# Scan branch of a decoder trunk: a new order for its gates, its state caches and its elementwise steps

## The chip, the cores and the metric

The kernel runs on one core of one Trainium2 chip. The metric is the device time of one execution in microseconds (us). A core has TensorE (PE) for matrix products, VectorE (DVE), ScalarE (ACT) and GpSimd (POOL) for elementwise work, and SyncE (SP), which here issues all bulk DMAs. Each engine works through its own queue in order; semaphores tie the queues together.

## The reference

Two layers, each an FFN half-step, a mixer and a second FFN half-step, on 288 columns: 256 prompt tokens and 8 samples of 4 tokens. The mixer has three branches; the change is in the second.

```python
h = rmsnorm(x);  u_pool, z, xbc, dt, q_mem, g = split(h @ w_in)
y_pool = pool_mix(u_pool)                      # branch 0: trailing windows 2/4/8/16
xs, B, C = silu(causal_conv(xbc))              # branch 1: Mamba-2 scan, 16 heads x 64, state 128
y, h_last = ssd_scan(xs, dt, a, B, C, h0)      # prompt: decays exp(seg); samples: h0 scaled, plus B x
y_ssm = grouped_rmsnorm((y + d_skip * xs) * silu(z)) * ssm_norm
y_mem = mem_attend(q_mem, k, v)                # branch 2: cross-attention
merged = sum_b sigmoid(g_b + bias_b) * (y_b @ w_br_b)
x = x + merged @ w_o
```

## The kernel before

**Weights.** All weights come in slabs of eight 128x128 tiles, 512 KB each, on SP's queue (`raw`). ACT copies a slab rounded into `whi` (L137) and DVE subtracts it from `raw` into `wlo` (L145). A tile is three products of 128x288 (`mm3`, L246): `whi` by the high part of the input, `whi` by its low part, `wlo` by the high part. So a slab is 24 products on PE.

**Order.** Nothing schedules at run time. `Stream.tick` runs ahead of every slab: it issues the load five slabs ahead, the split of the next slab, then `step()`, which takes one step of every work item on a list, in the list's order, then further splits. All small work (the scan, the attention, gates) is generators on this list; an item started with a delay `d` waits `d` slabs. What an item issues on PE stands ahead of the slab's own 24 products, as one burst.

**The mixer's slabs,** counted from the first `u` slab as r0: `u` r0 to r3, `z` r4 to r11, then per branch the gate columns g and the branch products b: g0/b0 r12 to r23, g2/b2 r24 to r35, g1/b1 r36 to r51, `o` r52 to r59. In each, b(c) follows two gates behind g(c).

**The scan's items.** `heads4(g)`, four of them, started with delays 4, 8, 12, 16: turn xs (`ps_x`), put the sums of the log decays in PSUM (`rows`, `ps_row`), scale by dt (`xd`, DVE) and by the decay to the end (`xw`, POOL), then per pair of heads clamp on DVE (`E<-ps_row,nact`, 128x512) and exponentials on ACT (`decay`), multiply by the masked C·B product (`E<-E,cbm`, DVE), products `ps_y`, finish (`xs<-xs,vec,ps_y`, `st`). `sample_state(b)`, eight of them, delays 8+2b: load a 512 KB state `hb`, mask B for the sample (`bm`, POOL), product `ps_yo` of the old state, scale the state by `Ee` (POOL, 128x1024), add the product `ps_up` (`hb<-hb,ps_up`, DVE), store. `sample_diag` (delay 7), `sample_y` (27) and `group_norm` (30; eight steps that end in the split inputs `ysh`, `ysl` of b1) follow.

**Shared buffers.** `xd`, `xw`, `bm`, the pooling branch's `pw` (POOL, L991 on), the attention's `pr` and `pp` come from one pool of five buffers of 128x512 ("t2"). PSUM has seven banks for all of this.

Of the kernel before, what the change touches and what calls it, by code (L numbers as in the profile page):

```python
# [15 lines left out]
KC = D // P  # L16
# [53 lines left out]
def mixer_groups():  # L70
    def w(kind, c, base, n=KC):
        return kind, (c,), [("w_in", base + c * P)], (n,)

    yield "q", (0, 1, 2, 3), [("w_in", C_Q + c * P) for c in range(4)], FIRST
    for c in list(range(8, 16)) + list(range(8)):
        yield w("xbc", c, C_XBC)
    for c in range(4):
        yield w("u", c, C_POOL)
    for c in range(8):
        yield w("z", c, C_Z)  # L80
    for br, name, n in ((0, "w_br_pool", 4), (2, "w_br_mem", 4), (1, "w_br_ssm", KC)):
        for c in range(KC + 2):
            if c < KC:
                yield w(f"g{br}", c, C_G + br * D)
            if c >= 2:
                yield f"b{br}", (c - 2,), [(name, (c - 2) * P)], (n,)
    yield "o", (0, 1, 2, 3), [("w_o", c * P) for c in range(4)], FIRST
    for c in range(4, 8):
        yield "o", (c,), [("w_o", c * P)], (KC,)
# [96 lines left out]
def trunk_kernel(ctx, tc, wpack, xT, memT, vecs, consts, wdt, wpool, hpool, hconv, h0T, kT, vC,  # L186
# [61 lines left out]
    def act(out, a, func, **kw):  # L248
        A.activation(out=out, in_=a, func=func, **kw)  # L249
# [344 lines left out]
    def mixer(i, cur, nxt):  # L594
# [65 lines left out]
        def dt_work(ps_dt):  # L660
# [71 lines left out]
            mm(pe[:, :TP], par, sb[32:32 + H, :])  # L732
            mm(pd[:, :P], ones[64:64 + H, :], sb[64:64 + H, :P])
            mm(pr[1][:, :TP], ones[96:96 + H, :], sb[96:96 + H, :])
            V.tensor_copy(out=nact[:, 0:2].rearrange("p a h -> p (a h)"), in_=pt[:, :2 * H])
            V.tensor_copy(out=nact[:TS, 2], in_=pt[:TS, 2 * H:3 * H])
            yield
            V.tensor_copy(out=Eb.rearrange("p a t -> p (a t)"), in_=pe[:, :256])
# [84 lines left out]
        def sample_state(b):  # L823
            hb = k4.tile([P, D], F32, tag="k4", name="hb")
            nc.sync.dma_start(out=hb, in_=h0T[i, b])
            yield
            bm = wide("bm", 96, 512, F32R)
            tt(bm, Bst.bitcast(F32), con[:96, K_BM + b:K_BM + b + 1].to_broadcast([96, 512]), ALU.mult, G)
            yield
            if b == 0:  # L830
                yo.append(sum_bank("ps_yo"))
            for g in range(4):
                mm(yo[0][TS * g:TS * g + TS, :256], block(cm, g, b), hb[:, g * 256:(g + 1) * 256], b == 0, b == DB - 1)
            h3 = hb.rearrange("p (h d) -> p h d", h=H)
            tt(h3, h3, Ee[:, b, :].unsqueeze(2).to_broadcast([P, H, 64]), ALU.mult, G)
            pu = [bank("ps_up0"), bank("ps_up1")]
            for g in range(4):
                mm(pu[g // 2][:, (g % 2) * 256:(g % 2 + 1) * 256], bm[:, g * P:(g + 1) * P],
                   xst[g // 2][:, (g % 2) * 256:(g % 2 + 1) * 256])
            yield  # L840
            if b == DB - 1:
                ysb = wide("ysb", P, 256)
                act(ysb, yo[0][:, :256], AF.Copy)
            for q in range(2):
                tt(hb[:, q * 512:(q + 1) * 512], hb[:, q * 512:(q + 1) * 512], pu[q], ALU.add)
            yield
            nc.sync.dma_start(out=o_ssm_s[i, b], in_=hb)
            if b == DB - 1:
                pt = bank("ps_yot")
                for j in range(2):  # L850
                    PE.transpose(pt[:, j * P:(j + 1) * P], ysb[:, j * P:(j + 1) * P], ident)
                yield
                Y4, E4 = (v.rearrange("p (g j) t -> p j g t", j=2) for v in (yoff, Eb))
                tt(Y4, pt[:, :256].rearrange("p (j g t) -> p j g t", j=2, g=4), E4, ALU.mult)

        def heads4(g):

            hs = slice(4 * g, 4 * g + 4)

            def rows(pi):  # L860
                prow = bank("ps_row")
                for j in range(2):
                    h = 4 * g + 2 * pi + j
                    mm(prow[:, j * TP:(j + 1) * TP], sel2[:, h:h + 1].to_broadcast([P, P]), nst)
                return prow

            def clamp(pi, prow):
                E = ep.tile([P, 2, 3 * P], F32, tag="E", name="E")
                h = 4 * g + 2 * pi
                nh = nact[:, 0:2, h:h + 2].rearrange("p t j -> p j t").unsqueeze(3).to_broadcast([P, 2, 2, P])  # L870
                tt(E.rearrange("p j (a t) -> p j a t", a=3)[:, :, 0:3:2, :],
                   prow.rearrange("p (j a t) -> p j a t", j=2, a=2), nh, ALU.max)
                return E

            def decay(pi, prow, E):
                for j in range(2):
                    h = 4 * g + 2 * pi + j
                    act(E[:, j, P:TP], prow[:, j * TP + P:(j + 1) * TP], AF.Exp, scale=-1.0, bias=b01[:, h:h + 1])
                    for t_ in range(2):
                        e = E[:, j, TP * t_:TP * t_ + P]  # L880
                        act(e, e, AF.Exp, scale=-1.0, bias=nact[:, t_, h:h + 1])

            def outputs(Es):

                ys = [bank("ps_y") for _ in Es]
                for pi, E in enumerate(Es):
                    for k in range(2):
                        for j in range(2):
                            x0 = k * TP + 128 * pi + 64 * j
                            mm(ys[pi][64 * j:64 * j + 64, k * P:TP], xd[:, x0:x0 + 64],  # L890
                               E[:, j, k * TP:k * TP + (2 - k) * P], k == 0, k == 1)
                for pi in range(2):
                    for k in range(2):
                        x0 = k * TP + 128 * pi
                        mm(ys[pi][:, 320:448], xw[:, x0:x0 + P], Bt[:, k, g * P:(g + 1) * P], k == 0, k == 1)
                return ys

            def finish(pi, py):
                p = 2 * g + pi
                xp = chunk(xsu, p)[:, :TP]  # L900
                st = tmp("st", P)
                stt(xp, xp, col(i, V_DS, p), py[:, :TP], ALU.mult, ALU.add)
                act(st, py[:, 320:448], AF.Copy)
                nc.sync.dma_start(out=o_ssm_p[i, p], in_=st)

            px = bank("ps_x")
            for t_ in range(2):
                for pi in range(2):
                    k = t_ * TP + pi * P
                    PE.transpose(px[:, k:k + P], chunk(xsu, 2 * g + pi)[:, t_ * P:(t_ + 1) * P], ident)  # L910
            r0 = rows(0)
            yield
            xd, xw = wide("xd"), wide("xw")
            xd4 = xd.rearrange("p (t h d) -> p t h d", t=2, h=4)
            tt(xd4, px.rearrange("p (t h d) -> p t h d", t=2, h=4),
               dtt[:, 0:2, hs].unsqueeze(3).to_broadcast([P, 2, 4, 64]), ALU.mult)
            tt(xw.rearrange("p (t h d) -> p t h d", t=2, h=4), xd4,
               wt[:, 0:2, hs].unsqueeze(3).to_broadcast([P, 2, 4, 64]), ALU.mult, G)
            E0 = clamp(0, r0)
            r1 = rows(1)  # L920
            yield
            E1 = clamp(1, r1)
            decay(0, r0, E0)
            decay(1, r1, E1)
            yield
            for E in (E0, E1):
                tt(E, E, cbm[:, g, :].unsqueeze(1).to_broadcast([P, 2, 3 * P]), ALU.mult)
            yield
            ys = outputs((E0, E1))
            yield  # L930
            finish(0, ys[0])
            finish(1, ys[1])
# [252 lines left out]
        for kind, cs, tiles, cuts in mixer_groups():  # L1185
# [9 lines left out]
                ym.extend(unit(f"ym{j}") for j in range(2))  # L1195
            if kind == "u" and c == 0:
                items["xss"] = W.start(xss_work(), 3)
                items["ss"] = [W.start(sample_state(b), 8 + 2 * b) for b in range(DB)]
                items["pairs"] = [W.start(heads4(g), 4 + 4 * g) for g in range(4)]
                items["pairs"].append(W.start(sample_diag(), 7))  # L1200
                items["yo"] = W.start(sample_y(), 27)
                items["gn"] = W.start(group_norm(), 30)
            if kind == "z" and c == 0:
                W.finish(items["conv"])
            if kind == "g2" and c == 0:
# [43 lines left out]
                items["dt"] = W.start(dt_work(ps_dt))  # L1249
            elif kind[0] == "g":  # L1250
                br = int(kind[1])
                gates[br, c] = tmp("gate")
                W.start(gate(br, c, ps[0], gates[br, c]))
            elif kind[0] == "b":
                W.start(merge(int(kind[1]), c, ps[0]))
            else:
                if norm is None:
                    norm = Norm(*nxt)
                W.start(x_update(cs, ps, norm))
# [125 lines left out]
```

## Time and profile before

| | us |
| --- | --- |
| median of three runs (lowest, highest) | 1559.61 (1558.95, 1559.99) |
| the profiled execution | 1559.71 |
| its span in the trace | 1557.6 |
| PE busy | 1533.0 (98%) |
| DVE busy | 1068.2 (69%) |
| ACT busy | 801.9 (51%) |
| POOL busy | 240.3 (15%) |

The span is the time from the first to the last instruction in the trace; the execution's own time is 2.1 us longer. Busy shares are averages over the FFN and mixer stages. Where an engine stood idle, the profile names what ended the idle time ("<-").

### The profile page before, as it was taken

What the parts mean: (1) busy time and instruction counts of PE and PEld (TensorE: products, weight loads), DVE (VectorE), ACT (ScalarE), POOL (GpSimd) and SP (SyncE); (2) the same over time, 40 slices, a digit from 0 to 9 for tenths busy, and PEclk for the clock granted to TensorE, in tenths of its full rate; (3) what the DMA queues carried; (4) which work ended last, traced back from release to release, by engine and by line L of the source; (5) the groups of instructions that cost most, each with busy time, mean ns of one, the idle gap of its engine ahead of it and who ended that gap; (6) DMA issues with size and microseconds to landing.
All of it is one profiled execution on the core that took longest, in us unless ns stands there. A gap on an engine that the chain in (4) does not pass through costs nothing.

```text
span 1557.6 us, 29192 instructions
## 1 busy us (share of the span) xinstructions
PE 1533.0 (98%) x11736; PEld 1492.8 (96%) x11736; DVE 1068.2 (69%) x1666; ACT 801.9 (51%) x1232; POOL 240.3 (15%) x324
## 2 busy tenths in 40 slices
PE   9999999999999999999999999999999999999997
PEld 7999999898889999999999999999988999999997
DVE  7766655898878767665566665579887776766643
ACT  7544444575655545444445444457556555544442
POOL 0100001245233111000000000024522310200001
PEclk9999999999999999999999999999999999999998
DMA  8644445565565545454545444546565655444551
GB/s 298 216 169 163 162 163 169 204 226 188 201 222 169 168 152 177 163 164 167 170 150 176 163 164 166 182 172 228 186 236 177 202 162 163 163 164 166 167 167 72
DMA packets 80711, 278.00 MB, mean 178 GB/s; under 512 B 9024, under 2 KB 13248, under 8 KB 80576
## 3 DMA queue, kind: packets, MB, share of 16 engines
q1 hardware_dynamic: 79872, 275.28, 52.4%
q8 instruction: 92, 1.51, 0.4%
q10 hardware_dynamic: 704, 0.86, 0.2%
q14 instruction: 43, 0.35, 0.1%
HBM read 262.39 MB, written 13.71 MB: 177 GB/s over the span
## 4 chain that ended last, share of the span: by engine, by line
PE 90%; DVE 5%; ACT 2%; POOL 1%; DMA 1%; issue 1%; DVEq 0%; ACTq 0%; POOLq 0%
PE ps L246 65%; PE pd L246 18%; PE ps_v L246 1%; POOL pw L234 1%; DVE wlo L145 1%; PE ps_y L246 1%; PE ps_k L246 1%; ACT whi L137 1%; DVE cacc L243 1%; PE ps_up L246 1%; PE ps_yo L246 1%; ACT L249 0%; DMA raw<-wpack 0%; PE ps_cb L246 0%; DVE E L234 0%
## 5 line engine op out<-in xcount | busy, mean ns | idle before, releaser
L145 DVE TENSOR_TENSOR wlo<-raw,whi 128x1024 fp32r<-128x1024 f32 (+1 forms) x441 | 551.6, 1252 | 257.7 <-ACT hidh L249 100.0
L137 ACT ACTIVATE whi<-raw 128x1024 fp32r<-128x1024 f32 (+1 forms) x441 | 464.0, 1054 | 313.9 <-PE ps L246 137.8
L246 PE MATMUL ps<-n1h,whi 128*128 128x288 f32 x896 | 270.4, 302 | 5.3 <-DVE cbuf L234 3.5
L246 PE MATMUL ps<-n1l,whi 128*128 128x288 f32 x896 | 264.9, 296 | 0.0
L246 PE MATMUL ps<-n1h,wlo 128*128 128x288 f32 x896 | 264.3, 295 | 0.6 <-DVE wlo L145 0.6
L246 PE MATMUL ps<-n2h,whi 128*128 128x288 f32 x704 | 208.8, 297 | 0.0
L246 PE MATMUL ps<-n0h,whi 128*128 128x288 f32 x704 | 208.8, 297 | 0.0
L246 PE MATMUL pd<-hidh,whi 128*128 128x288 f32 x704 | 208.4, 296 | 0.0
L246 PE MATMUL ps<-n2l,whi 128*128 128x288 f32 x704 | 207.7, 295 | 0.0
L246 PE MATMUL pd<-hidl,whi 128*128 128x288 f32 x704 | 207.7, 295 | 0.0
L246 PE MATMUL ps<-n0l,whi 128*128 128x288 f32 x704 | 207.7, 295 | 0.0
L246 PE MATMUL ps<-n0h,wlo 128*128 128x288 f32 x704 | 207.0, 294 | 0.0
L246 PE MATMUL ps<-n2h,wlo 128*128 128x288 f32 x704 | 207.0, 294 | 0.0
L246 PE MATMUL pd<-hidh,wlo 128*128 128x288 f32 x704 | 207.0, 294 | 0.0
L246 PEld LDWEIGHTS ps<-n1h,whi 128*128 128x128 f32 x896 | 168.7, 188 | 8.1 <-issue 5.1
L246 PEld LDWEIGHTS ps<-n1h,wlo 128*128 128x128 f32 x896 | 169.2, 189 | 0.8 <-DVE wlo L145 0.8
L246 PEld LDWEIGHTS ps<-n1l,whi 128*128 128x128 f32 x896 | 168.9, 189 | 0.5
L234 POOL TENSOR_TENSOR acc<-acc,sqr 128x288 f32<-128x288 f32 x42 | 45.9, 1092 | 797.4 <-ACT sqr L249 796.3
L246 PEld LDWEIGHTS pd<-hidh,wlo 128*128 128x128 f32 x704 | 132.6, 188 | 0.0
L246 PEld LDWEIGHTS ps<-n0h,wlo 128*128 128x128 f32 x704 | 132.6, 188 | 0.0
L246 PEld LDWEIGHTS ps<-n2h,wlo 128*128 128x128 f32 x704 | 132.6, 188 | 0.0
L246 PEld LDWEIGHTS ps<-n2l,whi 128*128 128x128 f32 x704 | 132.2, 188 | 0.1
(309 smaller groups left out, 2749.1 us busy)
## 6 DMA issues: line engine op xcount, KB each, us to landing
raw<-wpack SPq DMA_DIRECT2D x439, 512.0 KB, 3.3
cb<-kT SPq DMA_DIRECT2D x16, 512.0 KB, 5.6
cb<-vC SPq DMA_DIRECT2D x16, 512.0 KB, 4.7
hb<-h0T SPq DMA_DIRECT2D x16, 512.0 KB, 6.0
o_ssm_s<-hb SPq DMA_DIRECT2D x16, 512.0 KB, 5.0
x<-xT SPq DMA_DIRECT2D x4, 288.0 KB, 5.6
o_mk<-ksb SPq DMA_DIRECT2D x2, 512.0 KB, 5.7
o_mv<-vsb SPq DMA_DIRECT2D x2, 512.0 KB, 4.9
```

Source lines behind the costliest of these rows:

```text
L137: nc.scalar.activation(out=hi[:, a], in_=self.loaded[self.n_hi][:, a], func=AF.Copy)
L145: nc.vector.tensor_tensor(out=lo[:, a], in0=raw[:, a], in1=self.his[n][:, a].bitcast(F32), op=ALU.subtract)
L234: (eng or V).tensor_tensor(out=out, in0=a, in1=b, op=op)
L243: V.scalar_tensor_tensor(out=out, in0=a, scalar=s, in1=b, op0=op0, op1=op1)
L246: PE.matmul(out, lhsT=lhsT, rhs=rhs, start=start, stop=stop)
```

## The change

1. In the g1/b1 stage all eight gates go first (r36 to r43), then the eight products b1 (r44 to r51). Before, b1(0) stood at r39. The eight gates are kept in four buffers of the pool of units instead of the small temporaries.
2. Delays: `sample_diag` 7 to 6 and to the list's head, `heads4` 4+4g to 7+4g, `sample_state` 8+2b to 14+2b and behind the heads in the list, `sample_y` 27 to 33, `group_norm` 30 to 36.
3. From POOL to DVE: the scaling of the state (`hb<-hb,Ee`, 8 a layer) and `xw` (4 a layer). From POOL to ACT: `bm` (8 a layer).
4. From DVE to ACT: the clamp (8 a layer). `max(row, nact)` becomes four `Relu(row - nact)` of 128x128 straight from PSUM (`nact` is stored negated), and the four exponentials of these blocks become one of 128x512. The exponentials of the middle blocks stay. Both run in the step that made the rows' successor.

```diff
-    for br, name, n in ((0, "w_br_pool", 4), (2, "w_br_mem", 4), (1, "w_br_ssm", KC)):
-        for c in range(KC + 2):
+    for br, name, n, lag in ((0, "w_br_pool", 4, 2), (2, "w_br_mem", 4, 2), (1, "w_br_ssm", KC, KC)):
+        for c in range(KC + lag):
...
-            V.tensor_copy(out=nact[:, 0:2].rearrange("p a h -> p (a h)"), in_=pt[:, :2 * H])
+            ts(nact[:, 0:2].rearrange("p a h -> p (a h)"), pt[:, :2 * H], -1.0, ALU.mult)
...
-            tt(bm, Bst.bitcast(F32), con[:96, K_BM + b:K_BM + b + 1].to_broadcast([96, 512]), ALU.mult, G)
+            act(bm, Bst.bitcast(F32), AF.Copy, scale=con[:96, K_BM + b:K_BM + b + 1])
...
-            tt(h3, h3, Ee[:, b, :].unsqueeze(2).to_broadcast([P, H, 64]), ALU.mult, G)
+            tt(h3, h3, Ee[:, b, :].unsqueeze(2).to_broadcast([P, H, 64]), ALU.mult)
...
-                tt(E.rearrange("p j (a t) -> p j a t", a=3)[:, :, 0:3:2, :],
-                   prow.rearrange("p (j a t) -> p j a t", j=2, a=2), nh, ALU.max)
...
+                    for t_ in range(2):
+                        act(E[:, j, TP * t_:TP * t_ + P], prow[:, j * TP + P * t_:j * TP + P * t_ + P], AF.Relu,
+                            bias=nact[:, t_, h:h + 1])
                     act(E[:, j, P:TP], prow[:, j * TP + P:(j + 1) * TP], AF.Exp, scale=-1.0, bias=b01[:, h:h + 1])
-                    for t_ in range(2):
-                        e = E[:, j, TP * t_:TP * t_ + P]
-                        act(e, e, AF.Exp, scale=-1.0, bias=nact[:, t_, h:h + 1])
+                e = E.rearrange("p j (a t) -> p j a t", a=3)[:, :, 0:3:2, :]
+                act(e, e, AF.Exp, scale=-1.0)
...
-               wt[:, 0:2, hs].unsqueeze(3).to_broadcast([P, 2, 4, 64]), ALU.mult, G)
+               wt[:, 0:2, hs].unsqueeze(3).to_broadcast([P, 2, 4, 64]), ALU.mult)
...
-                items["ss"] = [W.start(sample_state(b), 8 + 2 * b) for b in range(DB)]
-                items["pairs"] = [W.start(heads4(g), 4 + 4 * g) for g in range(4)]
-                items["pairs"].append(W.start(sample_diag(), 7))
-                items["yo"] = W.start(sample_y(), 27)
-                items["gn"] = W.start(group_norm(), 30)
+                items["pairs"] = [W.start(sample_diag(), 6)] + [W.start(heads4(g), 7 + 4 * g) for g in range(4)]
+                items["ss"] = [W.start(sample_state(b), 14 + 2 * b) for b in range(DB)]
+                items["yo"] = W.start(sample_y(), 33)
+                items["gn"] = W.start(group_norm(), 36)
...
-                gates[br, c] = tmp("gate")
+                if br == 1 and c % 2 == 0:
+                    held = unit("gates")
+                gates[br, c] = held[:, c % 2, :] if br == 1 else tmp("gate")
```

**Place one: DVE's queue in slabs r4 to r6 of a layer,** where the pooling branch's windows (`pw` from POOL, `pd` on DVE) meet the scan's first heads. Before:

```order
L145 TENSOR_TENSOR wlo<-raw,whi 128x1024
L234 TENSOR_TENSOR xd<-ps_x,dtt 128x512
L234 TENSOR_TENSOR E<-ps_row,nact 128x2x2x128
L243 SCALAR_TENSOR_TENSOR pd<-pw,ub_4218 128x256
L243 SCALAR_TENSOR_TENSOR pd<-pw,ub_4218 128x32
L234 TENSOR_TENSOR pf<-pw,con 128x3
L234 TENSOR_TENSOR pd<-pf,ub_4218 128x3
L234 TENSOR_TENSOR z_4400<-ps,R_n_2450 128x288
L145 TENSOR_TENSOR wlo<-raw,whi 128x1024
L234 TENSOR_TENSOR xst_4339<-xss_4338,xst_4339 32x512
L234 TENSOR_TENSOR xst_4343<-xss_4342,xst_4343 32x512
L234 TENSOR_TENSOR E<-ps_row,nact 128x2x2x128
```

And now:

```order
L145 TENSOR_TENSOR wlo<-raw,whi 128x1024
L243 SCALAR_TENSOR_TENSOR pd<-pw,ub_4218 128x256
L243 SCALAR_TENSOR_TENSOR pd<-pw,ub_4218 128x32
L234 TENSOR_TENSOR pf<-pw,con 128x3
L234 TENSOR_TENSOR pd<-pf,ub_4218 128x3
L234 TENSOR_TENSOR z_4392<-ps,R_n_2450 128x288
L145 TENSOR_TENSOR wlo<-raw,whi 128x1024
L234 TENSOR_TENSOR xst_4339<-xss_4338,xst_4339 32x512
L234 TENSOR_TENSOR xst_4343<-xss_4342,xst_4343 32x512
L243 SCALAR_TENSOR_TENSOR pd<-pw,ub_4266 128x256
```

`xd` has left this place (it now stands at r8, behind all four `pd`), and the clamps `E<-ps_row,nact` are gone from DVE.

**Place two: DVE's queue from a scaling of attention weights (`pr`) in the g0/b0 stage,** with the state's adds (`hb<-hb,ps_up`) and the next heads. Before:

```order
L1037 RECIPROCAL sm<-sm 128x2
L238 TENSOR_SCALAR pr<-pr,sm 128x256 x2
L1030 TENSOR_REDUCE mx<-ps_sp 128x2
L238 TENSOR_SCALAR mx<-mx 128x2
L234 TENSOR_TENSOR hb<-hb,ps_up_4862 128x512
L234 TENSOR_TENSOR hb<-hb,ps_up_4863 128x512
L243 SCALAR_TENSOR_TENSOR xs_3001<-xs_3001,vec,ps_y 128x256 x2
L234 TENSOR_TENSOR xd<-ps_x,dtt 128x512
L234 TENSOR_TENSOR E<-ps_row,nact 128x2x2x128
L234 TENSOR_TENSOR gate<-ps,R_n_2450 128x288
L145 TENSOR_TENSOR wlo<-raw,whi 128x1024
```

And now:

```order
L1032 RECIPROCAL sm<-sm 128x2
L238 TENSOR_SCALAR pr<-pr,sm 128x256 x2
L1025 TENSOR_REDUCE mx<-ps_sp 128x2
L238 TENSOR_SCALAR mx<-mx 128x2
L234 TENSOR_TENSOR gate<-ps,R_n_2450 128x288
L145 TENSOR_TENSOR wlo<-raw,whi 128x1024
L243 SCALAR_TENSOR_TENSOR xs_3001<-xs_3001,vec,ps_y 128x256 x2
L234 TENSOR_TENSOR xd<-ps_x,dtt 128x512
L234 TENSOR_TENSOR xw<-xd,wt 128x512
L234 TENSOR_TENSOR hb<-hb,Ee 128x1024
L234 TENSOR_TENSOR part_4956<-ps,gate 128x288
L145 TENSOR_TENSOR wlo<-raw,whi 128x1024
```

The next heads' steps and the state's adds have moved from the slab of `pr` to its neighbours, and `xw` and the scaling `hb<-hb,Ee` stand on DVE.

**Place three: ACT's queue at a group's decays.** Before, the first group's (at r6):

```order
L249 ACT_TABLE_LOAD
L249 ACTIVATE E<-ps_row,b_3008 128x128
L249 ACTIVATE E<-E,nact 128x128 x2
L249 ACTIVATE E<-ps_row,b_3008 128x128
L249 ACTIVATE E<-E,nact 128x128 x2
L249 ACTIVATE E<-ps_row,b_3008 128x128
L249 ACTIVATE E<-E,nact 128x128 x2
L249 ACTIVATE E<-ps_row,b_3008 128x128
L249 ACTIVATE E<-E,nact 128x128 x2
L137 ACTIVATE whi<-raw 128x1024
```

And now, from the first group's first pair (at r8):

```order
L249 ACTIVATE E<-ps_row,nact 128x128 x2
L249 ACT_TABLE_LOAD
L249 ACTIVATE E<-ps_row,b_3008 128x128
L249 ACTIVATE E<-ps_row,nact 128x128 x2
L249 ACTIVATE E<-ps_row,b_3008 128x128
L249 ACTIVATE E<-E 128x2x2x128
L249 ACTIVATE yph_4135<-ps_pool,vec 128x288
L137 ACTIVATE whi<-raw 128x1024
L249 ACTIVATE E<-ps_row,nact 128x128 x2
```

A pair of heads now has seven activations instead of six, one of them four blocks wide, and its two pairs stand in two slabs instead of one. The program's loads of activation tables go from 48 to 52.

## Rows read from the trace of the kernel before

**Rows 1.** PE's waits by line waited for: us in total, times, longest us.

```profile
PE ps L246 <- DVE cbuf L234: 3.5, 2, 1.8
PE ps_y L246 <- DVE E L234: 3.1, 2, 1.9
PE ps_row L246 <- DVE hb L234: 2.2, 2, 1.1
PE ps L246 <- DVE hb L234: 1.8, 2, 0.9
PE ps_row L246 <- DVE xs L234: 1.5, 1, 1.5
...
PE ps L246 <- DVE wlo L145: 0.6, 1, 0.6
```

**Rows 2.** PE's timeline, first layer, slab r7: start, us, instruction, [idle before <-releaser].

```profile
376.53 0.51 PE L246 MATMUL ps<-n1h,whi 128*128 128x288 f32 x1
376.87 0.29 PE L246 MATMUL ps<-n1l,whi 128*128 128x288 f32 x1
377.75 0.40 PE L246 MATMUL ps<-n1h,wlo 128*128 128x288 f32 x1 [0.58 <-DVE wlo L145]
377.98 0.30 PE L246 MATMUL ps<-n1h,whi 128*128 128x288 f32 x1
...
380.65 0.29 PE L246 MATMUL ps<-n1h,wlo 128*128 128x288 f32 x1
382.87 2.02 PE L246 MATMUL ps_y<-E,xd 128*64 128x256 f32 x16 [1.93 <-DVE E L234]
```

**Rows 3.** Windows: length; busy us (instructions) by engine; granted clock, DMA share, GB/s.

```profile
384.37:387.78 3.41, 3.41 (x19) 2.77 (x15) 3.20 (x12) 0.96 (x2) 0.00 (x0) 0.50 0.60 196
410.70:458.37 47.67, 46.55 (x358) 41.73 (x359) 38.23 (x59) 35.24 (x71) 14.17 (x10) 1.00 0.55 191
1053.75:1057.16 3.41, 3.41 (x15) 3.41 (x16) 3.34 (x9) 2.21 (x5) 1.93 (x5) 0.55 0.90 347
```

**Rows 4.** DVE's and POOL's timelines, first layer, slabs r3 to r7.

```profile
359.84 1.74 POOL L234 TENSOR_TENSOR pw<-ub 128x422 f32<-128x422 f32 x1
...
366.28 0.89 POOL L234 TENSOR_TENSOR pw<-ub 128x422 f32<-128x422 f32 x1
...
372.67 0.69 DVE L234 TENSOR_TENSOR xd<-ps_x,dtt 128x512 f32<-128x512 f32 x1 [6.62 <-POOL pw L234]
...
379.04 0.69 DVE L234 TENSOR_TENSOR E<-ps_row,nact 128x512 f32<-128x512 f32 x1
```

**Rows 5.** DVE's and POOL's timelines at the same moment of the g0/b0 stage.

```profile
406.25 2.90 DVE L238 TENSOR_SCALAR pr<-pr,sm 128x256 f32<-128x256 f32 x2
406.05 1.90 POOL L234 TENSOR_TENSOR hb<-hb,Ee 128x1024 f32<-128x1024 f32 x1 [5.59 <-PE ps_yo L246]
```

**Rows 6.** Groups by line and shape, first layer's r0 on: count | busy, mean ns | idle before.

```profile
L145 DVE TENSOR_TENSOR wlo<-raw,whi 128x1024 fp32r<-128x1024 f32 x47 | 59.8, 1273 | 3.0 <-PE ps L246 2.4 <-ACT whi L137 0.6
L234 POOL TENSOR_TENSOR hb<-hb,Ee 128x1024 f32<-128x1024 f32 x8 | 16.4, 2055 | 48.5 <-PE ps_yo L246 48.5
L249 ACT ACT_TABLE_LOAD x10 | 12.8, 1283 | 4.7 <-PE ps_pv L246 3.2 <-DVE rs L240 1.1 <-issue 0.3
L249 ACT ACTIVATE E<-E,nact 128x128 f32<-128x128 f32 x32 | 11.0, 398 | 0.0
L238 DVE TENSOR_SCALAR pr<-pr,sm 128x256 f32<-128x256 f32 x8 | 10.1, 1296 | 0.1
L234 POOL TENSOR_TENSOR bm<-Bst,con 96x512 fp32r<-96x512 f32 x8 | 8.5, 1063 | 0.3 <-ACT E L249 0.3
L243 DVE SCALAR_TENSOR_TENSOR ysl<-z,vec,ysh 128x288 fp32r<-128x288 f32 x8 | 4.7, 646 | 0.0
L234 POOL TENSOR_TENSOR xw<-xd,wt 128x512 f32<-128x512 f32 x4 | 4.4, 1089 | 21.8 <-DVE xd L234 21.8
L249 ACT ACTIVATE z<-z 128x576 f32<-128x576 f32 x4 | 2.4, 674 | 0.0
```

More of the change, by code (lines that the diff above doesn't have):

```diff
@@ L80, in mixer_groups @@
         yield w("z", c, C_Z)
-    for br, name, n in ((0, "w_br_pool", 4), (2, "w_br_mem", 4), (1, "w_br_ssm", KC)):
-        for c in range(KC + 2):
+    for br, name, n, lag in ((0, "w_br_pool", 4, 2), (2, "w_br_mem", 4, 2), (1, "w_br_ssm", KC, KC)):
+        for c in range(KC + lag):
             if c < KC:
                 yield w(f"g{br}", c, C_G + br * D)
-            if c >= 2:
-                yield f"b{br}", (c - 2,), [(name, (c - 2) * P)], (n,)
+            if c >= lag:
+                yield f"b{br}", (c - lag,), [(name, (c - lag) * P)], (n,)
     yield "o", (0, 1, 2, 3), [("w_o", c * P) for c in range(4)], FIRST
@@ L865, in rows, with decay @@
                 return prow
-            def clamp(pi, prow):
+            def decay(pi, prow):
                 E = ep.tile([P, 2, 3 * P], F32, tag="E", name="E")
-                h = 4 * g + 2 * pi
-                nh = nact[:, 0:2, h:h + 2].rearrange("p t j -> p j t").unsqueeze(3).to_broadcast([P, 2, 2, P])
-                tt(E.rearrange("p j (a t) -> p j a t", a=3)[:, :, 0:3:2, :],
-                   prow.rearrange("p (j a t) -> p j a t", j=2, a=2), nh, ALU.max)
-                return E
-            def decay(pi, prow, E):
                 for j in range(2):
                     h = 4 * g + 2 * pi + j
+                    for t_ in range(2):
+                        act(E[:, j, TP * t_:TP * t_ + P], prow[:, j * TP + P * t_:j * TP + P * t_ + P], AF.Relu,
+                            bias=nact[:, t_, h:h + 1])
                     act(E[:, j, P:TP], prow[:, j * TP + P:(j + 1) * TP], AF.Exp, scale=-1.0, bias=b01[:, h:h + 1])
-                    for t_ in range(2):
-                        e = E[:, j, TP * t_:TP * t_ + P]
-                        act(e, e, AF.Exp, scale=-1.0, bias=nact[:, t_, h:h + 1])
+                e = E.rearrange("p j (a t) -> p j a t", a=3)[:, :, 0:3:2, :]
+                act(e, e, AF.Exp, scale=-1.0)
+                return E
             def outputs(Es):
@@ L917, in heads4 @@
             tt(xw.rearrange("p (t h d) -> p t h d", t=2, h=4), xd4,
-               wt[:, 0:2, hs].unsqueeze(3).to_broadcast([P, 2, 4, 64]), ALU.mult, G)
-            E0 = clamp(0, r0)
+               wt[:, 0:2, hs].unsqueeze(3).to_broadcast([P, 2, 4, 64]), ALU.mult)
+            E0 = decay(0, r0)
             r1 = rows(1)
             yield
-            E1 = clamp(1, r1)
-            decay(0, r0, E0)
-            decay(1, r1, E1)
+            E1 = decay(1, r1)
             yield
```

## Prediction

> **What bounds the kernel now.** I began with the table of busy times: PE is busy 1533.0 us of a span of 1557.6, so the elementwise engines matter only where PE waits for them. Second came PE's waits by line [rows 1]. The reader should see that not all of them are in reach. The 3.5 us for `cbuf` belong to the convolution, which the change leaves alone. The other five rows shown (E, hb twice, xs, wlo; eight waits in two layers) lie in the stretch that is rewritten: 3.1 + 2.2 + 1.8 + 1.5 + 0.6 = 9.2 us.
>
> Third, PE's timeline around the worst of them, to see what a wait costs from start to start [rows 2]. Products follow each other every 0.133 us (from 377.98 to 380.65 twenty steps), so a slab of 24 is 3.2 us. From 380.65 to 382.87 it is 2.22 us, that is 2.09 lost, where the row names 1.93: idle time is counted from a modelled end, 0.16 behind the pitch. Eight waits therefore cost 9.2 + 8 x 0.16 = **10.5 us**.
>
> Fourth, the granted clock in windows [rows 3]. Just behind the 2-us wait of layer 0, TensorE ran 3.41 us at 0.50, the lower of its two levels (1.2 GHz); before it PE had idled. The same work at full clock takes half, so this costs **1.7 us**. A second stretch, 3.41 us at 0.55, follows the untouched convolution wait of layer 1.
>
> Fifth, why DVE is late. Two causes show. In r5 and r6 DVE stands 6.62 us until POOL finishes `pw` [rows 4]: `xd` needs a buffer of the pool that the windows `pw` fill, and everything behind it, the clamps, the next `wlo`, E, is late by as much. Later, in the attention's slabs, the two scalings `pr` of 128x256 take 2.90 us, and the first of them begins 0.2 us after POOL's state scaling, which runs 1.90 us [rows 5]. An operation of 128x512 takes 0.69 on DVE [rows 4], so a 128x256 should need about 0.4 (an estimate from that row and the 1.27 of 128x1024); the eight average 1.296 [rows 6]. These slabs also carry the state's adds and the next heads in the old order, and the `hb` waits of PE stand right behind.
>
> **The change, part by part.**
>
> *Later heads.* `xd` goes to r8, behind all four `pd`, where POOL's windows are over. DVE then waits for POOL only in `pd`, one `pw` chain at a time, and `wlo` is not behind the last chain. That removes the E and `wlo` waits of layer 0 and the E and xs waits of layer 1: 3.1 + 1.5 + 0.6, with four times 0.16 5.8 us, and the clock's 1.7 with the wait ahead of it. Next late in these slabs is POOL's own chain: the same operations in the same slabs, and the products that need it (`ps_pool`) are in their old places. For that I keep 0.5 us a layer, **+1.0** in all; the ends are 0 (no wait shows at `ps_pool` in rows 1) and half of the 5.8.
>
> *POOL's work to DVE and ACT.* Per layer DVE gets 8 scalings of 128x1024 at 1.27 (the row of `wlo`, same size [rows 6]) and 4 `xw` at 0.69 [rows 4]: 10.2 + 2.8. It loses 8 clamps at 0.69, 5.5, and if `pr` falls from 1.296 to 0.4 in eight cases, 7.2. The sum is near zero, +0.3 us a layer, against 16.4 + 8.5 + 4.4 that POOL no longer needs [rows 6]. What counts is the spread: by the order, the adds, heads and scalings now stand in different slabs than `pr`. So the four `hb` waits (2.2 + 1.8 + four times 0.16 = 4.6 us) go. Bounds: if `pr` stays at 1.296 for a reason of its own, DVE has +7.5 a layer; in the window of 47.67 us that is 38.23 + 7.5 = 45.7 at the most [rows 3], still below the window.
>
> What covers the DVE's scaling: the old state's product `ps_yo` must read `hb` before it is scaled, so DVE waits there for PE's burst of the same slab. Behind it in DVE's queue stand a gate or part and the `wlo` for two slabs on. POOL's idle of 48.5 us behind `ps_yo` [rows 6] shows that this wait is real where nothing precedes it; on DVE earlier work of the slab covers part. `wlo` is made two slabs ahead, 6.4 us, so I cost it at nothing, and at up to 2 us a layer if it is not.
>
> *ACT.* Per pair of heads it has four more activations at up to 0.398 and, for the four single exponentials, one of 128x512, at most 0.674 (the row of 128x576 [rows 6]): +0.67, times 8 is 5.4 a layer. `bm` at no more than 0.674, times 8, 5.4. Two more table loads a layer, 2.6 [rows 6]. Together 13.3 us. In the busiest window ACT has 35.24 of 47.67 [rows 3]; even if all 13.3 fell there it would be 48.5, and in its slabs, r12 to r20, stand three of eight `bm` and no more than three of four groups. So I take no loss; the upper bound is 0.9 us a layer, more if an operation costs more than its row.
>
> *Bursts on PE.* By the order the number of products is the same, but outputs, rows and state now come in more separate slabs. Returning from an fp32 product to the slab's own costs 0.34 from 376.53 to 376.87 [rows 2], 0.21 above the pitch. I count four more returns a layer: 8 x 0.21 = **+1.7 us**. The bounds are 0 and six a layer, 2.5.
>
> *Gates first.* The stage has the same 16 slabs. The norm chain moves by six slabs (delay 30 to 36), but b1(0) only by five (r39 to r44): one slab of reserve goes, the only one that there was between r37 and r39. I cost it at nothing: the last step's four `ysl` take 4 x 0.646 = 2.6 us [rows 6] and start with slab r43; b1(0) needs its group 3 at its seventh tile, 3.2 + 2.4 = 5.6 us later.
>
> *SP's queue.* The state loads are moved by six slabs past weight loads of the same size and number; at 0.55 DMA share in the window [rows 3] I cost that at nothing. The state's stores end six slabs later, still ahead of `o`.
>
> **Sum.** 1559.71 - 10.5 - 1.7 + 1.0 + 1.7 = 1550.2. The profiled execution is 0.1 above the median of the runs, so this stands for the median as well.
>
> **The rivals.**
>
> *The windows still hold PE.* DVE no longer stands idle in r5 and r6, and POOL's window additions then run beside DVE operations with two inputs. The same addition of 128x422 took POOL 0.89 us while DVE stood idle and 1.74 while it worked [rows 4]. If the last two windows' seven additions each lose that 0.85, POOL is 6 us later, about what `xd` waited; `pd` and the `wlo` behind it are then as late as now, and the waits of r5 to r8 (5.8) and the clock's 1.7 stay under other names: 1550.2 + 7.5 = 1557.7, no change that can be told. Against it: DVE has only some 4 us of work in those slabs, so no more than two or three additions meet it, and each `pd` needs one chain alone. 9%. It holds as well for a change that doesn't free `xd`.
>
> The Trainium skill, "SBUF — State Buffer", "Who interferes with whom", says that DVE and GpSimd share a pair of ports as an exclusive lock, and that whoever starts first blocks the other for its whole instruction. Rows 5 agree: the `pr` pair ends 1.2 us behind POOL's scaling, having begun 0.2 behind its start. By that rule every addition that meets DVE loses what is left of a DVE operation, which is this rival's 1557.7.
>
> *ACT becomes the pacing engine* (the slower side). Place: r12 to r20 and the slabs behind. If its moved operations cost f times my 13.3, ACT needs 35.24 + 13.3 f against PE's 47.67 there; it decides from f = 0.93 if all fall into the window, from 1.5 if three fifths do. At f = 1.5 with all of it there: 55.2, 7.5 us a layer, 1550.2 + 15 = 1565. `whi` would come late and PE wait by it. Against it: no row of rows 1 names `whi`, and relu of a 128x128 block has a near row. 5%. A milder form, 2 to 3 us a layer, gives 1555; 9%.
>
> The Trainium skill, "ScalarE: Activation LUTs", "What ACT_TABLE_LOAD costs", adds a drain of 1.38 us to each table load of 1.28. The row has 1.283 for the load [rows 6]; no row shows the drain. By it ACT would get 4 x 1.38 = 5.5 us more in the two layers, and the sum would be about 1551 to 1556 where ACT is short, the mild form above.
>
> *The norm chain is late for b1(0).* One slab of slip, 3.2 us, less the 1.7 that 5.6 - 2.6 and one `wlo` leave, is 1.5 us; with a stretch of half clock behind it 1.7 more; in both layers 6.4: 1556.6, within the bound of no change. It decides from 1.7 us of slip. 5%.
>
> *More than the eight waits*: if the half clock behind layer 1's convolution does not come this time, at most half of 3.41 more goes [rows 3], and with no extra bursts and no rest at the windows it would be 1550.2 - 1.7 - 1.7 - 1.0 = 1545.8. 4%.
>
> **How the numbers follow.** Forecast 1550.2 (own range 1547 to 1553.5) 68%; larger gain 4%; mild ACT loss, 1555, 9%; windows 9%; norm chain 5%; ACT pacing 5%. The range from 1546 to 1556.5 leaves out the windows, the norm chain and ACT pacing, 19%. A measurement of this kernel can tell about 0.2% from no change, 3.1 us. Faster by more than that (below 1556.5): 68 + 4 + 9 = 81%. Within: 9 + 5 = 14%. Slower: 5%.
>
> **What would show it.** PE's waits for E, hb, xs and `wlo` should be gone in both layers, the 0.50 window behind 384 us too, and `cbuf` should stay at 3.5. `pr` should take about 0.4 each. DVE's idle in r5 and r6 should be for `pd`, under 3 us at a time. ACT's busy time should grow by about 27 us, POOL's fall by about 59 (29.3 a layer). A wait of PE for `whi` would be the ACT rival, one for `ysl` or `z` at b1(0) the norm chain, one for `pd` or `ps_pool` the windows. I am wrong if PE's busy sum grows by more than 3 us, or if waits of the same sum stand at other lines.

## The result, and the profile after

The changed kernel takes 1549.72 us (median; 1548.65 to 1550.64), against 1559.74 for the kernel before; the ratio is 0.9936, with a 95% interval from 0.9919 to 0.9954. Beside the later runs it was timed once more: 1550.94 us, ratio 0.9946 (0.9932 to 0.9959). One of those five runs was in a slower state (1598.32 us) and is left out of the ratio. The profiled execution, 1548.65, is the fastest of its four, 1.1 below their median. The prediction was 1550.2, between 1546 and 1556.5. The number came out; two of the reasons behind it did not.

The busy times of the changed kernel:

```profile
span 1546.9 us, 29125 instructions
PE 1529.1 (99%) x11736; PEld 1490.6 (96%) x11736; DVE 1065.0 (69%) x1674; ACT 824.6 (53%) x1268; POOL 190.8 (12%) x284
```

Of the 10.7 us that the span lost, PE's busy time accounts for only 3.9; the rest was idle time. What PE still waits for, by line (us in total, times, longest):

```profile
PE ps L246 <- DVE cbuf L234: 3.5, 2, 1.8
PE ps L246 <- DVE gate L234: 2.1, 2, 1.0
...
PE ps_s L246 <- DMA cb<-kT: 0.6, 1, 0.6
```

Against [rows 1], E, hb, xs and `wlo` are gone from the mixers, `cbuf` is untouched, and a new line has come: PE waits for DVE's eviction of a gate, once a layer. Its place in layer 0, by the timelines of PE, then DVE (start, us, instruction, idle before):

```profile
440.79 0.64 PE L246 MATMUL ps_yo<-hb,cm 128*32 128x256 f32 x8
441.36 0.74 PE L246 MATMUL ps_up<-xst,bm 96*128 96x256 f32 x4
443.14 0.40 PE L246 MATMUL ps<-n1h,whi 128*128 128x288 f32 x1 [1.04 <-DVE gate L234]
```

```profile
437.08 0.69 DVE L234 TENSOR_TENSOR xw<-xd,wt 128x512 f32<-128x512 f32 x1
441.50 1.22 DVE L234 TENSOR_TENSOR hb<-hb,Ee 128x1024 f32<-128x1024 f32 x1 [3.72 <-PE ps_yo L246]
442.64 0.45 DVE L234 TENSOR_TENSOR gate<-ps,R_n 128x288 f32<-128x288 f32 x1
```

Read it from below. PE's next product needs the PSUM bank that the eviction at 442.64 empties. The gate's product had been done long before; but in DVE's queue the eviction stands behind the scaling of the state, and the scaling stands 3.72 us until PE has read the old state (`ps_yo`). DVE waits for PE's burst, and then PE waits for DVE: 1.04 by the row, 1.2 from start to start.

A good ruler for all runs is the time on PE's timeline from the first product of slab r0 to the first of slab r55. It leaves out what the start of the program and the convolution do.

| kernel | layer 0 | layer 1 |
| --- | --- | --- |
| before | 226.58 | 224.94 |
| changed | 220.93 | 220.53 |

So 5.65 us were gained in layer 0 and 4.41 in layer 1, 10.06 of the 10.7; the remainder lies between the two stretches.

### The profile page after: what moved, and what is told of

Its sections match the earlier page's. It is cut to its first block, busy times and chain, and to the rows that moved or that the text cites. A ratio compares the mean times of both kernels' runs of the same rounds, so it can differ in the third digit from the quotient of the medians.

```text
span 1546.9 us, 29125 instructions
## 1 busy us (share of the span) xinstructions
PE 1529.1 (99%) x11736; PEld 1490.6 (96%) x11736; DVE 1065.0 (69%) x1674; ACT 824.6 (53%) x1268; POOL 190.8 (12%) x284
## 4 chain that ended last, share of the span: by engine, by line
PE 95%; DVE 2%; DMA 1%; ACT 1%; issue 1%; ACTq 0%; DVEq 0%
PE ps L246 67%; PE pd L246 18%; PE ps_v L246 1%; PE ps_y L246 1%; PE ps_k L246 1%; PE ps_up L246 1%; PE ps_yo L246 1%; PE ps_av L246 0%; DVE cacc L243 0%; DMA raw<-wpack 0%; PE ps_sp L246 0%; PE ps_pv L246 0%; DVE wlo L145 0%; PE ps_cb L246 0%; ACT whi L137 0%
## 5 line engine op out<-in xcount | busy, mean ns | idle before, releaser
L246 PEld LDWEIGHTS ps<-n0l,whi 128*128 128x128 f32 x704 | 132.1, 188 | 0.1
```

What stands on the lines that cost most here:

```text
L246: PE.matmul(out, lhsT=lhsT, rhs=rhs, start=start, stop=stop)
```

## The experiments

My theory was that each part of the change removes its own waits: the later heads those of r5 to r8, the moves off POOL (through `pr`) and the new spread those for hb. Rival 1 said that the order does it all, rival 2 that the engines do.

### The order alone, the engines alone

The first run keeps the new delays and the gates first, with everything on its old engine; the second keeps the old order and moves only the engines.

```diff
 # order alone, against the changed kernel
-            act(bm, Bst.bitcast(F32), AF.Copy, scale=con[:96, K_BM + b:K_BM + b + 1])
+            tt(bm, Bst.bitcast(F32), con[:96, K_BM + b:K_BM + b + 1].to_broadcast([96, 512]), ALU.mult, G)
-            tt(h3, h3, Ee[:, b, :].unsqueeze(2).to_broadcast([P, H, 64]), ALU.mult)
+            tt(h3, h3, Ee[:, b, :].unsqueeze(2).to_broadcast([P, H, 64]), ALU.mult, G)
...
```

> The changed kernel with all work on its old engines: state scaling, xw and masked B on POOL, clamp on DVE; only the new delays and gates first are left. Theory (each half of the change removes its own waits): the waits for E, xs and wlo in slabs r5 to r8 are gone with the half clock behind them, 5.8 + 1.7 us, and the new wait for a gate's bank (2.1 us by the row, 2.4 with the pitch) is gone too, since POOL scales the state; but pr is stretched wherever POOL scales beside it, so part of the hb waits (up to 4.6) stays: 1549 to 1554. Rival 1 (the order does it all): no wait left, about 1547.5. Rival 2 (the engines do it all): about 1559.

> The kernel before with only the engines changed: state scaling and xw on DVE, masked B, clamp and merged exponential on ACT; old delays, old place of the gates. Theory: xd still stands behind POOL's windows, so the 6.6 us of idle DVE and the E, xs and wlo waits stay (5.8 + 1.7); pr falls to about 0.35 and the hb waits (4.6) go, but DVE has state scaling, adds, heads and pr in the same slabs, so some new wait may come: 1555 to 1559. Rival 1 (the order does it all): 1559.7 or more. Rival 2 (the engines do it all): 1549.7.

Measured: the order alone 1548.73 us, ratio 0.9932 (0.9919 to 0.9944), stretches 219.71 and 219.77. The engines alone 1561.38, ratio 1.0013 (1.0004 to 1.0022), stretches 224.88 and 226.76: if anything slower than before. Rival 1 stands, and my share for the engines falls. The order alone is 1.2 and 0.8 us shorter in the stretches than the changed kernel, and PE waits in one place a layer:

```profile
PE ps_pv L246 <- DVE xd L234: 0.4, 2, 0.2
```

The engines alone are 1.7 us shorter in layer 0 and 1.8 longer in layer 1 than the kernel before. In layer 1 PE waits 2.15 us for E and xs, in layer 0 only 0.42; why the layers differ stays open. PE's waits with the engines alone:

```profile
PE ps L246 <- DVE hb L234: 2.6, 2, 1.3
PE ps L246 <- DVE gate L234: 2.1, 2, 1.1
PE ps_row L246 <- DVE xs L234: 2.0, 2, 1.6
...
PE ps_y L246 <- DVE part L234: 1.3, 2, 0.6
...
PE ps_row L246 <- DVE hb L234: 1.1, 2, 0.5
```

The hb waits are there, 2.6 and 1.1 against 1.8 and 2.2 in [rows 1], though POOL no longer disturbs `pr`. DVE's groups, `pr` with the engines alone and then with the order alone:

```profile
L238 DVE TENSOR_SCALAR pr<-pr,sm 128x256 f32<-128x256 f32 x8 | 2.5, 351 | 0.1
```

```profile
L238 DVE TENSOR_SCALAR pr<-pr,sm 128x256 f32<-128x256 f32 x8 | 3.7, 503 | 0.2
```

`pr` takes 351 ns where no POOL work meets it and 1296 in [rows 6]; that part of the reading was right. But at 351 the hb waits stay, at the same two products a layer, and in the order alone they are gone with one `pr` a layer still stretched to 1.1 us beside POOL's masked B. So a short `pr` is not enough to remove these waits, and a stretched one is not enough to make them.

That the stretch had no part in them is not shown. With the engines alone DVE does the state's scaling ahead of the same adds, and that can make them late as well. In the kernel before the adds stand behind a `pr` pair of 2.47 us, where an undisturbed pair takes 0.62. The difference of 1.85 is more than PE's wait of 1.12 (PE, then DVE):

```profile
429.39 0.74 PE L246 MATMUL ps_up<-xst,bm 96*128 96x256 f32 x4
434.23 0.50 PE L246 MATMUL ps_row<-nst,sel 128*128 128x256 f32 x2 [1.12 <-DVE hb L234]
```

```profile
430.21 2.47 DVE L238 TENSOR_SCALAR pr<-pr,sm 128x256 f32<-128x256 f32 x2
433.49 1.28 DVE L234 TENSOR_TENSOR hb<-hb,ps_up 128x512 f32<-128x512 f32 x2
```

### The new gate wait

```diff
 # scaling later, against the changed kernel
-            h3 = hb.rearrange("p (h d) -> p h d", h=H)
-            tt(h3, h3, Ee[:, b, :].unsqueeze(2).to_broadcast([P, H, 64]), ALU.mult)
             pu = [bank("ps_up0"), bank("ps_up1")]
...
             yield
+            h3 = hb.rearrange("p (h d) -> p h d", h=H)
+            tt(h3, h3, Ee[:, b, :].unsqueeze(2).to_broadcast([P, H, 64]), ALU.mult)
             for q in range(2):
                 tt(hb[:, q * 512:(q + 1) * 512], hb[:, q * 512:(q + 1) * 512], pu[q], ALU.add)
```

> The changed kernel with the state's scaling on DVE moved one step later, right ahead of the adds of the same state. Theory (the new wait of 1.04 us a layer at slab r20 comes from DVE standing 3.7 us in front of the scaling until PE's product of the old state is through, with the eviction of a gate's bank queued behind it): both gate waits go, 2.4 us, about 1547.3, and DVE no longer stands idle for ps_yo. Rival (PSUM banks are short there whatever DVE does): the wait stays or moves to another bank's release, 1549.7.

> The changed kernel with only the state's scaling back on POOL. Theory (POOL's scaling stretches pr where they meet, and DVE's scaling makes the new gate wait): the gate waits go (2.4 us), pr beside a scaling takes over 1 us again, and since pr and the adds no longer share a slab little of it reaches PE: 1547 to 1550. Rival (the move to DVE is what removed the hb waits): PE's waits for hb are back, up to 4.6 us, 1552 to 1554.

Measured: scaling later 1547.84, ratio 0.9927 (0.9913 to 0.9940), stretches 219.11 and 219.12. Scaling on POOL 1546.58, ratio 0.9921 (0.9909 to 0.9934), stretches 219.07 and 218.95. In neither does PE wait once inside the two stretches. The waits with the scaling on POOL, down to the first line that belongs to the end of the program:

```profile
PE ps L246 <- DVE cbuf L234: 3.5, 2, 1.8
PE ps_still L246 <- DVE still L515: 1.5, 1, 1.5
```

So the gate wait came from the place of the scaling in DVE's queue, as the two rows at 441.50 and 442.64 say, and not from a shortage of banks. The scaling on POOL has the lowest median of all versions; the intervals of the scaling later and of the heads at 8+4g (below) overlap with its own. Against the changed kernel timed on the same terms (0.9946) its interval overlaps a little, but the stretches differ by 3.7 us, 438.0 against 441.75. It also stretches `pr` again, to 639 ns on the mean, and PE does not notice:

```profile
L238 DVE TENSOR_SCALAR pr<-pr,sm 128x256 f32<-128x256 f32 x8 | 4.8, 639 | 0.1
```

### Which delay does it

```diff
 # heads alone, against the kernel before
-                items["pairs"] = [W.start(heads4(g), 4 + 4 * g) for g in range(4)]
-                items["pairs"].append(W.start(sample_diag(), 7))
+                items["pairs"] = [W.start(sample_diag(), 6)] + [W.start(heads4(g), 7 + 4 * g) for g in range(4)]
                 items["ss"] = [W.start(sample_state(b), 8 + 2 * b) for b in range(DB)]
```

> The kernel before with only the heads' delays (7+4g) and the diagonal's (6), both ahead of the states in the list; states, norm chain, gates and all engines as before. Theory now (each delay removes the waits of its own items): the waits for E, xs and wlo and the half clock at 384 go, 5.8 + 1.7 us, since xd stands behind POOL's windows no more; the states' adds still share slabs with pr, so hb waits of some size stay: 1550 to 1554. Rival (one cure for all: what matters is only that heads and states stand apart): no wait left, about 1547.5.

> The kernel before with the states' delays (14+2b), sample_y 33, norm chain 36 and the gates first; the heads at 4+4g and all engines as before. Theory: the waits for E, xs and wlo in r5 to r8 stay with their half clock (5.8 + 1.7), the four hb waits (4.6) go: 1554 to 1556. Rival (one cure for all): about 1547.5; rival that the adds are late because of pr under POOL's scaling: hb waits stay, 1559.

Measured: the heads alone 1548.38, ratio 0.9938 (0.9925 to 0.9952), stretches 220.86 and 220.23. The states alone (with the gates first) 1555.56, ratio 0.9977 (0.9968 to 0.9986), stretches 223.11 and 223.06. The heads' and the diagonal's delays with their new place in the list give all that the whole change gives. I had expected 1550 to 1554 for them, with hb waits; most of these are gone. The states alone came out in the expected range, but one of the two hb waits a layer stayed. PE's waits with the heads alone, the two lines that belong to the stretches:

```profile
PE ps_x L910 <- DVE hb L234: 0.7, 2, 0.3
...
PE ps L246 <- DVE xd L234: 0.2, 1, 0.2
```

And with the states alone:

```profile
PE ps_row L246 <- DVE xs L234: 2.9, 2, 1.5
PE ps_row L246 <- DVE hb L234: 2.1, 2, 1.0
...
PE ps_y L246 <- DVE E L234: 1.0, 2, 0.5
```

The later heads remove the early waits and most of the hb waits; the later states remove one hb wait a layer and shorten E.

Was it the phase of the heads to the slabs of `pr` (period four), or that they are later and stand ahead of the states in the list? One more slab restores the old phase:

```diff
-                items["pairs"] = [W.start(sample_diag(), 6)] + [W.start(heads4(g), 7 + 4 * g) for g in range(4)]
+                items["pairs"] = [W.start(sample_diag(), 6)] + [W.start(heads4(g), 8 + 4 * g) for g in range(4)]
```

> As the run with the heads' delays alone, but 8+4g instead of 7+4g: one slab later still, and in the same phase to the attention's and the states' slabs (period 4 and 2) as the 4+4g of before. Theory (the waits of r5 to r8 went because the heads come behind POOL's windows; the hb waits went because the heads' steps left the slabs of pr and the adds): the early waits stay gone, hb waits of some 1 us each are back, 1550 to 1554. Rival (only lateness matters): 1548.4 as with 7+4g.

Measured: 1547.35, ratio 0.9927 (0.9914 to 0.9939), stretches 219.83 and 219.11, no hb wait at all, where I had expected 1550 to 1554. My theory of the phase falls too. PE's only new wait there is for a state's load:

```profile
PE ps_yo L246 <- DMA hb<-h0T: 0.7, 1, 0.7
```

What is left as a reason for the hb waits can be read in the program's order, and no run tested it. Which of the seven PSUM banks a product gets is fixed there. In the kernel before, the row product at 434.23 takes the bank of the state's `ps_up0`, made ahead of it in the same burst. The first of DVE's two adds frees that bank (433.49, 0.69 long), behind `pr` and a reduction. With the heads at 8+4g, and ahead of the states in the list, the row product stands ahead of `ps_up` in its burst and takes a bank that the attention's softmax emptied before. Nor is `pr` stretched there (PE, then DVE):

```profile
424.32 0.48 PE L246 MATMUL ps_row<-nst,sel 128*128 128x256 f32 x2
425.30 0.73 PE L246 MATMUL ps_up<-xst,bm 96*128 96x256 f32 x4
```

```profile
422.90 0.62 DVE L238 TENSOR_SCALAR pr<-pr,sm 128x256 f32<-128x256 f32 x2
```

In another slab of that run a `pr` pair of 2.30 us stands ahead of the adds, and PE does not wait:

```profile
412.23 2.30 DVE L238 TENSOR_SCALAR pr<-pr,sm 128x256 f32<-128x256 f32 x2
```

Whether the later start or the place in the list changed the banks, these runs do not separate.

### The buffer that xd waited for

```diff
-    up = ctx.enter_context(tc.tile_pool(name="up", bufs=30))
+    up = ctx.enter_context(tc.tile_pool(name="up", bufs=29))
...
-    t2 = ctx.enter_context(tc.tile_pool(name="t2", bufs=5))
+    t2 = ctx.enter_context(tc.tile_pool(name="t2", bufs=6))
```

> The kernel before with six instead of five buffers in the pool that xd, xw and the pooling windows share (one buffer of the units fewer, to make room). Theory (xd waited for a buffer that POOL's windows held): DVE's idle of 6.6 us in front of xd shrinks, the E, xs and wlo waits go or shrink by the one addition that is no longer waited for (about 1 us of each, 4 of 5.8) and the half clock with them: 1552 to 1557. Rival (POOL's chain itself is late and pd carries the wait): DVE stands as long in front of pd, 1559.

Measured: 1558.4, ratio 0.9997 (0.9988 to 1.0006), stretches 226.29 and 224.59. The gain that I had expected (1552 to 1557) did not come. DVE's rows there, then PE's wait:

```profile
371.34 0.69 DVE L234 TENSOR_TENSOR xd<-ps_x,dtt 128x512 f32<-128x512 f32 x1 [5.65 <-POOL pw L234]
371.95 0.68 DVE L234 TENSOR_TENSOR E<-ps_row,nact 128x512 f32<-128x512 f32 x1
372.55 1.25 DVE L243 SCALAR_TENSOR_TENSOR pd<-pw,ub 128x256 f32<-128x256 f32 x2
373.72 0.27 DVE L234 TENSOR_TENSOR pf<-pw,con 128x3 f32<-128x3 f32 x1
374.03 0.97 DVE L234 TENSOR_TENSOR pd<-pf,ub 128x3 f32<-128x3 f32 x1
...
378.41 0.69 DVE L234 TENSOR_TENSOR E<-ps_row,nact 128x512 f32<-128x512 f32 x1
```

```profile
382.24 1.83 PE L246 MATMUL ps_y<-E,xd 128*64 128x256 f32 x16 [1.93 <-DVE E L234]
```

The buffer was the reason for the idle time: one more takes one addition of 0.97 us out of 6.62 [rows 4]. But DVE now meets POOL's last additions, and a `pd` of three columns lasts 0.97. In the kernel before it lasted 0.16:

```profile
375.47 0.16 DVE L234 TENSOR_TENSOR pd<-pf,ub 128x3 f32<-128x3 f32 x1
```

The gain is spent on that: the second clamp begins only 0.63 us earlier (379.04 in [rows 4]), of which 0.36 is an earlier start of the whole stretch (345.62 against 345.98), and PE's wait in front of E is 1.93 as before (in layer 1 0.83 against 1.19). A third of a microsecond a layer is all that reaches the stretches. This is the rival "the windows still hold PE" in small, and it is real; the full change escapes it, and by its order no step of the heads stands behind the windows any more.

### Reserves: ACT, the norm chain, the gates

```diff
 # more work for ACT, against the changed kernel
             act(bm, Bst.bitcast(F32), AF.Copy, scale=con[:96, K_BM + b:K_BM + b + 1])
+            act(bm, Bst.bitcast(F32), AF.Copy, scale=con[:96, K_BM + b:K_BM + b + 1])
```

> The changed kernel with the masked B made twice, that is one more activation of 96x512, 0.71 us by the trace, in each of eight slabs a layer: 5.7 us more for ACT a layer. Theory (ACT had reserve, it paces nothing): no more than 1 us longer, 1549 to 1551, no wait of PE for whi, E or bm. Rival (ACT was the next engine in line): up to 5.7 us a layer where slabs are full, 1553 to 1560.

Measured: 1552.1, ratio 0.9952 (0.9940 to 0.9965), stretches 221.63 and 221.43. The median is above the expected 1549 to 1551, though the interval overlaps with that of the changed kernel. Of the 5.7 us a layer that ACT got, PE pays 0.6 to 0.9, in one place, where `pp` is late:

```profile
PE ps_up L246 <- ACT pp L249: 1.6, 2, 0.8
```

ACT is not the pacing engine, but it has almost nothing left at that one spot: a wait appears with 0.7 us more a slab.

```diff
 # norm chain later, against the changed kernel
-                items["gn"] = W.start(group_norm(), 36)
+                items["gn"] = W.start(group_norm(), 37)
```

> The changed kernel with the norm chain's delay 37 instead of 36, one slab later, which takes more than the reserve ahead of b1(0). By the prediction's sum (1.7 us to spare) PE waits 1.5 us or more a layer at b1(0), 1552.5 to 1556; if the chain has over 3.2 us to spare, nothing shows, 1549.7. A wait names ysl, ysh or z.

Measured: 1550.77, ratio 0.9942 (0.9929 to 0.9956), stretches 220.93 and 220.84, no wait at b1(0). In the changed kernel the last `ysl` are made long before the tile that needs them:

```profile
527.79 1.80 DVE L243 SCALAR_TENSOR_TENSOR ysl<-z,vec,ysh 128x288 fp32r<-128x288 f32 x4
...
531.66 0.30 PE L246 MATMUL ps<-ysh,whi 128*128 128x288 f32 x1
```

They end at 529.59, and b1(0) needs them 2.4 us behind 531.66, at 534.06: 4.5 us of reserve, not 1.7.

> The kernel before with only the gates of g1/b1 first and kept in the pool of units; delays and engines as before. Theory (the same 16 slabs in another order cost nothing and bring nothing by themselves): 1559.2, the eight waits unchanged. Rival: the norm chain of before, with its one slab to spare at b1(0), was a hidden wait, then up to 1 us faster.

Measured for the gates first alone (the loop and the buffers of that part of the diff, on the kernel before): 1559.35, ratio 1.0000 (0.9991 to 1.0009), stretches 226.52 and 224.81. As forecast, nothing.

> The changed kernel once more beside the others on one chip, to set it against the run with the state scaling on POOL (1546.6) and the one with the scaling later (1547.8): theory 1549 to 1550, 2.4 us above them by the two gate waits; rival: the same as they.

Measured: the numbers given with the result, stretches 220.94 and 220.81. The gate wait of 1.2 and about 0.7 us a layer more separate it from the run with the scaling on POOL. Of the 0.7, 0.28 stands in one burst of the same products, which takes 3.92 us from 417.39 here and 3.64 from 418.22 there; where the rest goes stays open.

## Why the prediction was right, step by step

**The early waits** (5.8 us): right. They went, and they went with the heads' delay and place in the list, for the reason given.

**The half clock behind 384 us** (1.7): right in the sum, wrong as a separate term. The run with the gates alone has layer 0 as in the kernel before, but without that fall. Its window and the same one of the kernel before (length; busy us by engine; granted clock third from the end):

```profile
382.67:388.00 5.33, 3.76 (x31) 2.87 (x32) 5.09 (x17) 2.46 (x5) 0.00 (x0) 1.00 0.75 212
```

```profile
382.87:388.20 5.33, 5.24 (x31) 4.13 (x32) 5.09 (x17) 2.46 (x5) 0.00 (x0) 0.68 0.70 218
```

The same 31 products take the same 5.33 us, at 1.00 or at 0.68, and the whole stretches are equal too, 226.52 and 226.58. At full clock PE gets there earlier and waits for `xs` instead, as layer 1 did all along in [rows 1]:

```profile
387.50 0.47 PE L246 MATMUL ps_row<-nst,sel 128*128 128x256 f32 x2 [1.48 <-DVE xs L234]
```

The slow clock of layer 0 and the xs wait of layer 1 are one and the same delay: DVE's. Had only the clock been mended, nothing would have been gained.

**The hb waits** (4.6): they went, but the step that failed is the cause. I put them on `pr` stretched by POOL, and on heads and adds in the slabs of `pr`. The engines alone make `pr` short and keep the waits, 3.7 of 4.0 us. The heads at 8+4g bring a head's row product back beside a `pr`, and there is no wait. What the runs show is that the heads' start and place in the program's order remove most of the waits; that this works through the banks is read from the order and not tested.

**POOL's work to DVE** (costed at nothing, at up to 2 us a layer otherwise): mis-sized. It cost 1.2 us a layer by the gate wait, and 1.9 in the stretches, by the repeat against the run with the scaling back on POOL. I named what stood behind the waiting scaling, a gate and `wlo`, and took `wlo` as the one that counts, since it is two slabs ahead. The gate's eviction is the one: it holds a bank that PE needs within the slab.

**Bursts** (+1.7) and **the rest at the windows** (+1.0): neither shows. PE's timeline has 25 bursts in a layer's stretch instead of 22, three more and not four, and the sum comes out without a charge for them. Layer 0 lost 5.16 us of waits and 1.7 of slow clock and got 1.2 back, which makes 5.66; measured 5.65. Layer 1: 5.31 less 1.2 is 4.11; measured 4.41. With the scaling on POOL, where no wait is left, the stretches gained 7.51 and 5.99, even 0.65 and 0.68 more than the waits and the slow clock. These two surcharges stood where the gate wait of 2.4 should have stood, so the sum of 1550.2 is near the 1549.72 partly by luck; the repeat came to 1550.94.

**ACT** (no loss, busy time up by 27): no loss; up by 22.7. The masked B takes 720 ns instead of at most 674, and the merged exponential 682:

```profile
L249 ACT ACTIVATE bm<-Bst,con 96x512 fp32r<-96x512 f32 x8 | 5.8, 720 | 0.0
L249 ACT ACTIVATE E<-E 128x512 f32<-128x512 f32 x8 | 5.5, 682 | 0.0
```

The Trainium skill, "ScalarE: Activation LUTs", "What ACT_TABLE_LOAD costs", gives 280 ns and 0.833 an element for an activation with a pointer operand, an estimate of 707 for 512 elements; the 720 agrees better with it than my row. The drain of 1.38 us that the section adds to a table load does not show here: the load begins where ACT's last instruction ends, it takes 1.28, and the next activation begins 1.30 behind its start.

```profile
408.61 0.20 ACT L249 ACTIVATION_READ_ACCUMULATOR pr<-ps_sp,mx 128x1 f32 x1
408.82 1.28 ACT L249 ACT_TABLE_LOAD   x1
410.12 0.96 ACT L249 ACTIVATE gate<-gate,vec 128x288 f32<-128x288 f32 x2
```

**POOL** was to fall by 59 and fell by 49.5. What stayed on it took 9 us longer. The window additions `pw` of 128x416, for one, took 1742 ns on the mean instead of 1097, now that DVE works beside them. That much of the rival "the windows still hold PE" came, but PE waited for none of it. DVE, costed at 0.3 us a layer more, was busy 1.6 less.

**Gates first** at nothing: right by its own run. The reserve of the norm chain was mis-sized, 4.5 us where I had 1.7.

## What to carry to other kernels

Ask of every operation that you hand to another engine not how long it takes but where its queue will stand still, and which of the things queued behind it frees a bank or a buffer that the bounding engine needs next. Try the order of the program before the division of labour: new delays for the heads and a new place in the list gave here what the whole change gave, and the moved operations by themselves gave nothing or less. And where a slow clock and a wait follow each other, look for a stretch with the same wait at full clock before you count both.

## What the hardware showed that was not expected

The fall of the clock at the convolution's wait is not a property of the program. That wait is 1.75 to 1.78 us long in all fourteen profiles, twice in each. In 17 of the 28 cases a stretch of 3.41 us at 0.5 goes with it, in 11 none: in the profiled run of the kernel before only in layer 1 [rows 3], in that of the changed kernel in neither, in its repeat in layer 1, with the order alone in both. From the end of the wait to r0, PE takes 39.65 to 39.82 us with the fall, in either layer; without it, 38.3 in layer 0 and 38.9 to 39.3 in layer 1. So one fall costs about 1.5 us in layer 0 and 0.4 to 0.9 in layer 1, which is as much as the smaller effects of this study; the stretches from r0 to r55 were needed to see them.
